# A top-2 MoE router moved ahead of its layer norm: un-normalised logits, an affine part applied at the gathers' copies, and 20 weight places in place of 23

## The chip, the cores and the metric

One core of one Trainium2 chip runs the whole network in one launch. The metric is device microseconds of that launch. The engines are PE (TensorE: matmuls, transposes), DVE (VectorE), ACT (ScalarE), POOL (GpSimd) and SP, whose queue here only issues weight loads from HBM.

## The reference, cut to what matters

Two layers of mixer, layer norm, mixture of experts and layer norm, then two other blocks (a recurrent and a sliding-window one, each with a dense FFN), which the change does not touch. T = 256 tokens, D = 1024, 16 experts of width 512, all in fp32.

```python
mix = hybrid_mixer(x, ...)                    # ends in  concat(heads) @ w_o
x = layer_norm(ALPHA * x + mix, ln1_g[l], ln1_b[l])
aff = sigmoid(x @ router_w)                   # 16 affinities for each token
biased = aff + router_bias
# best group of 4 by the sum of its two largest, then the two largest in that group
gates = chosen affinities over their sum
out = sum over the chosen experts of  gate * (silu(x @ w_gate[e]) * (x @ w_up[e])) @ w_down[e]
x = layer_norm(ALPHA * x + out, ln2_g[l], ln2_b[l])
```

## The kernel before, in words

Tokens stand in two blocks b of 128 rows, and an fp32 product is made from high and low fp32r parts (`xh`, `xl`; `wh`, `wl`): three matmuls for one. `mm` (L174) issues every matmul, `tr` (L228) every transpose.

**The mixer's end.** `down` multiplies the heads with `w_o` into four PSUM tiles `y[b][q]`, q being a half of 512 columns, one after the other. `layer_norm` (L362 for all DVE work) adds the residual, takes moments, and applies scale, gain and bias in two SCALAR_TENSOR_TENSOR passes for each (b, q). `xT_part` transposes the normalised `xn` on PE (`pt`) and splits it into `xh` (ACT, L332) and `xl` (DVE, L333). `warm` (L224) issues matmuls on constants to keep PE at work; twelve stand here.

**The router.** `logits` (`plt`) multiplies `xh`, `xl` with the split router weights `rwhl`; the 32x128 result is copied (`lg`, L838), turned and added up by one small matmul (`psg`), and goes through the sigmoid (L861), the bias add on DVE (L862) and some 25 small DVE instructions to a 0/1 choice `selb` (L886). PE counts ranks in each expert from it (`prk`), DVE forms a one-hot matrix `P` (L1023) of 64 slots for each expert.

**The experts.** Meanwhile ACT and POOL write the split of `xn` with strided columns, `xnh` (L980) and `xnl` (L981). `slots(g)` gathers the tokens of four experts: eight PSUM tiles `pg`, each of four matmuls of `P` with `xnh`, `xnl`, copied out in turn by DVE (L1037) and ACT (L1035) into `xTe`; then four `pgt` transposes and eight `pgs` matmuls. The four PSUM tiles of tag "pb" rotate under all of these. Then for eight pairs p of experts: `gate_up(p)` (`pgg`, `pgu`), `down()` of the pair before (`pdn`), `turn` (`pat`), `spread` (`py`, the sum in four PSUM tiles that begin as ALPHA times `xn`, written by four ACT instructions, L989). `slots(1)` to `slots(3)` stand between the pairs. PE's order there is the program's (`manual_schedule`).

**The weights.** A layer has 96 chunks of 1 MB, each two SP loads of 512 KB (`chunks`, L147). One string says where the first go, ahead of need:

```python
FILL = "rrrmr76rr54rr321rrp0ppx"
LATE = 18
```

Here `r` is a ring buffer, a digit a place of its own, `p` a pair of `xh`, `xl` buffers (three pairs rotate), `m` the tile `misc`, `x` the tile `xn`. That is 23 chunks; `m` holds the fourth chunk in use and is loaded after 18 others. From then on the 18 places of `r` and the digits are used in a cycle, each as soon as its chunk has been multiplied. SP issues strictly in order.

Of the kernel before, what the change touches and what calls it, by code (L numbers as in the profile page):

```python
# [19 lines left out]
D = 1024  # L20
# [13 lines left out]
WARM_LN = 12  # L34
# [63 lines left out]
class Net:  # L98
# [4 lines left out]
    FILL = "rrrmr76rr54rr321rrp0ppx"  # L103
# [153 lines left out]
    def more_consts(s):  # L257
# [8 lines left out]
        s.col = s.cp.tile([128, 32], F32, name="col")  # L266
        t = s.raw()
        rows, rw = t[:32, 0:128], t[:, 128:256].rearrange("p (k e) -> p k e", k=8)
# [4 lines left out]
        rv = A["router_w"].rearrange("(k p) e -> p k e", p=128)  # L273
        for k in (0, 4):
            nc.gpsimd.dma_start(rw[:, k:k + 4], rv[:, k:k + 4])
        return rows, rw

    def columns(s, rows, rw):
        nc = s.nc
        p = s.pb()  # L280
        keep = s.tc.keep_in_program_order
        keep(s.tr(p[:, :27], rows[:27]))
        keep(nc.vector.tensor_copy(s.col[:, :27], p[:, :27]))
        s.rwhl = s.cp.tile([128, 8, 32], F32R, name="rwhl")
        h = s.rwhl[:, :, 0:16]
        keep(nc.scalar.activation(h, rw, AF.Copy))
        keep(nc.vector.tensor_tensor(s.rwhl[:, :, 16:32], rw, h.bitcast(F32), op=ALU.subtract))
# [60 lines left out]
    def layer_norm(s, y, gb, out=None, added=False, after0=None):  # L348
# [38 lines left out]
        with s.tc.high_priority():  # L387
# [6 lines left out]
            if after0:  # L394
                s.warm(WARM_LN)
            else:
                lows((0, 0), (0, 1))
            for q in range(2):
                affine(1, q)
            if after0:  # L400
                lows((0, 0), (1, 0), (0, 1))
                after0()
                lows((1, 1))
            else:
                lows((1, 0), (1, 1))
# [115 lines left out]
    def mixer(s, li):  # L521
# [6 lines left out]
        with ExitStack() as es:  # L528
# [26 lines left out]
            place([128, 1152], "gap2", 1)  # L555
# [12 lines left out]
            for i in range(2):  # L568
                nc.gpsimd.dma_start(alb[64 * i:64 * i + 4], A["alib"][i])
            if li == 0:  # L570
                rows = s.more_consts()
# [35 lines left out]
            if li == 0:  # L607
                s.columns(*rows)
# [156 lines left out]
            gb = s.load_gb(mp, A["ln1_g"][li], A["ln1_b"][li], "kT")  # L765
# [5 lines left out]
            s.lg = []  # L771
            s.down(mh, ml, A["w_o"][li], 8, gb,
                   after0=lambda: s.lg.append(s.logits(0)))

    def down(s, mh, ml, w, nk, gb, col=None, out=None, hold=4, after0=None, pre=None, pool=()):
# [24 lines left out]
        if out is None:  # L800
            s.xh, s.xl = s.new_xT()
# [6 lines left out]
        s.layer_norm(y, gb, out, after0=after0)  # L808
# [19 lines left out]
    def logits(s, b):  # L828
# [4 lines left out]
        for k in range(8):  # L833
            s.mm(p, s.rwhl[:, k], s.xh.k(k, t), k == 0, False)
        for k in range(8):
            s.mm(p[:16], s.rwhl[:, k, 0:16], s.xl.k(k, t), False, k == 7)
        lg = s.st.tile([32, 128], F32, tag="lg", name="lg", bufs=2)
        s.nc.vector.tensor_copy(lg, p)  # L838
        return lg

    def router(s, mp):
# [12 lines left out]
        v.memset(pick, -BIG_NEG)  # L854
        v.memset(gs[:, 0], BIG_NEG)
        s.tc.keep_in_program_order(nc.scalar.activation(sm[:, 0], s.eps, AF.Sigmoid))
        s.lg.append(s.logits(1))
        p = s.pb("psg")
        for b in range(2):
            s.mm(p[:, b * 16:(b + 1) * 16], s.lg[b], s.two, True, True)  # L860
        nc.scalar.activation(R[:, 0], p[:, :32], AF.Sigmoid)  # L861
# [47 lines left out]
        return ga, ov, rs, cnt  # L909

    def overflow(s, li, ga, ov, rs, cnt, xnh, xnl, py):
# [7 lines left out]
        with s.tc.If(n > 64), ExitStack() as es:  # L919
# [4 lines left out]
            for c in range(8):  # L924
# [5 lines left out]
                v.tensor_copy((x0, x1)[c // 4][:, c % 4], p[:, :T])  # L930
# [27 lines left out]
    def moe(s, li, pre):  # L958
        nc, A = s.nc, s.A
        v = nc.vector  # L960
        with ExitStack() as es:
# [14 lines left out]
            keep = s.tc.keep_in_program_order  # L976
            for b in range(2):
# [498 lines left out]
```

## Time and profile before

| what | value |
|---|---|
| median of 3 runs | 1370.97 us (1370.66 to 1371.42) |
| the profiled execution's own time | 1371.13 us |
| its span | 1369.5 us |
| mean granted clock of TensorE | 0.983 |
| PE busy | 1306.6 us (95%) |
| DVE, ACT, POOL busy | 763.1, 583.2, 81.0 us |
| moved from HBM | 340 MB, 249 GB/s on the mean |

Times in rows count from the span's start. The router of layer 0 lies between 126 and 162 us, its experts between 162 and 370; layer 1's router ends 362 us later. A row gives a start, a duration, the engine, the line, what is written and from what, the shapes, how many instructions were merged, and in brackets the idle time before it on its engine with what ended that.

### The profile page before, as it was taken

The page shows a single profiled execution, that of the slowest core. Times are in us where ns is not written, and L with a number is a line of the kernel's source. Part 1 is how long each engine was busy: PE and PEld are TensorE (multiplying, and loading weights), DVE is VectorE, ACT ScalarE, POOL GpSimd, SP SyncE. Part 2 cuts the span into 40 slices and gives each one's busy share as a digit, 9 for nine tenths or more (in the row PEclk, how much of TensorE's full clock was granted, in tenths as well). Part 3 has the DMA queues.
Part 4 walks back from the last instruction along what each step waited for, and adds up shares of the span by engine and source line. Part 5 has one row for each costly group of instructions (what it writes and reads, how often), then busy time and mean ns, then how long its engine had stood idle before and what let it go on. Part 6 is the DMA issues. An engine that isn't in the chain of part 4 may idle for free.

```text
span 1369.5 us, 20419 instructions
## 1 busy us (share of the span) xinstructions
PE 1306.6 (95%) x7941; PEld 955.6 (70%) x7941; DVE 763.1 (56%) x1584; ACT 583.2 (43%) x1110; POOL 81.0 (6%) x90
## 2 busy tenths in 40 slices
PE   7899899999998998999998999999999999999997
PEld 6787443444487664434435888889998887899986
DVE  4775510111368562111115678879886678888845
ACT  5684410101256841101103524556665376566642
POOL 3000100000200010000002143000000010000000
PEclk9999999999999999999999999999999999999999
DMA  9566699999981767999998820466554365575500
GB/s 299 192 236 256 240 408 398 416 418 416 324 304 70 277 244 290 393 416 417 417 416 290 287 96 29 157 214 214 185 202 136 126 216 171 181 234 185 199 18 31
DMA packets 153448, 342.93 MB, mean 250 GB/s; under 512 B 13282, under 2 KB 84840, under 8 KB 153345
## 3 DMA queue, kind: packets, MB, share of 16 engines
q1 hardware_dynamic: 149408, 330.14, 65.4%
q0 software_dynamic: 3616, 11.15, 2.4%
q8 instruction: 66, 1.08, 0.3%
q10 hardware_dynamic: 320, 0.26, 0.1%
q14 instruction: 38, 0.30, 0.1%
HBM read 340.44 MB, written 1.07 MB: 249 GB/s over the span
## 4 chain that ended last, share of the span: by engine, by line
PE 52%; DVE 3%; ACT 1%; issue 1%; DMA 0%; POOL 0%; DVEq 0%; ACTq 0%
PE pb L174 20%; PE y L174 12%; PE pv L174 3%; PE pdn L174 3%; PE pgg L174 3%; PE pgu L174 3%; PE pl L174 2%; PE ptk L174 2%; DVE xn L362 1%; PE py L174 1%; PE pkv L174 1%; PE po L174 1%; PE pt L228 1%; PE pg L174 1%; DVE wl L168 1%
## 5 line engine op out<-in xcount | busy, mean ns | idle before, releaser
L168 DVE TENSOR_TENSOR wl<-raw,wh 128x1024 fp32r<-128x1024 f32 (+1 forms) x208 | 248.3, 1199 | 86.2 <-ACT wh L167 84.3
L167 ACT ACTIVATE wh<-raw 128x1024 fp32r<-128x1024 f32 (+1 forms) x208 | 213.7, 1035 | 70.2 <-PE y L174 62.1
L1067 DVE SCALAR_TENSOR_TENSOR misc<-misc,gs,pgu 128x512 f32<-128x512 f32 x16 | 12.0, 747 | 226.8 <-PE pgu L174 149.8
L174 PE MATMUL pb<-xh,wh 128*128 128x256 f32 (+1 forms) x944 | 133.6, 281 | 0.5 <-ACT wh L167 0.5
L174 PE MATMUL pb<-xh,wl 128*128 128x256 f32 (+1 forms) x944 | 132.5, 281 | 1.6 <-DVE wl L168 1.6
L174 PE MATMUL pb<-xl,wh 128*128 128x256 f32 (+1 forms) x944 | 132.5, 280 | 0.0
L174 PEld LDWEIGHTS pb<-xh,wh 128*128 128x128 f32 (+1 forms) x944 | 120.3, 187 | 2.1 <-ACT wh L167 0.7
L174 PEld LDWEIGHTS pb<-xh,wl 128*128 128x128 f32 (+1 forms) x944 | 119.9, 187 | 2.2 <-DVE wl L168 2.0
L174 PEld LDWEIGHTS pb<-xl,wh 128*128 128x128 f32 (+1 forms) x944 | 119.9, 187 | 0.1
L174 PE MATMUL pgu<-raw,xTe 128*64 128x512 f32 x512 | 112.6, 592 | 0.0
L174 PE MATMUL pdn<-raw,misc 128*64 128x512 f32 x496 | 109.6, 592 | 0.0
L174 PE MATMUL pgg<-raw,xTe 128*64 128x512 f32 x448 | 103.0, 612 | 4.9 <-PEq L919 4.9
L167 ACT ACTIVATE xh<-pdn 128x512 fp32r<-128x512 f32 x32 | 19.1, 597 | 195.6 <-PE pdn L174 195.6
L174 PEld LDWEIGHTS pgu<-raw,xTe 128*64 128x64 f32 x512 | 37.7, 137 | 72.2 <-issue 68.7
L174 PEld LDWEIGHTS pdn<-raw,misc 128*64 128x64 f32 x496 | 36.4, 137 | 69.4 <-issue 64.4
L174 PEld LDWEIGHTS pgg<-raw,xTe 128*64 128x64 f32 x448 | 32.8, 140 | 65.1 <-issue 58.7
L168 DVE TENSOR_TENSOR xl<-pdn,xh 128x512 fp32r<-128x512 f32 x32 | 21.9, 686 | 100.4 <-ACT xh L167 88.5
L174 PE MATMUL y<-wl,gh 128*128 128x512 f32 x176 | 68.7, 390 | 0.0
L174 PE MATMUL y<-wh,gl 128*128 128x512 f32 x176 | 68.6, 390 | 0.0
L174 PE MATMUL y<-wh,gh 128*128 128x512 f32 x176 | 68.2, 389 | 0.0
L1066 ACT ACTIVATE misc<-pgg 128x512 f32<-128x512 f32 x16 | 9.6, 597 | 128.0 <-PE pgg L174 128.0
L174 PE MATMUL y<-wh,xl 128*128 128x512 f32 x128 | 51.4, 403 | 0.0
(357 smaller groups left out, 2267.1 us busy)
## 6 DMA issues: line engine op xcount, KB each, us to landing
raw<-in_w_up SPq DMA_DIRECT2D x128, 512.0 KB, 9.9
raw<-in_w_down SPq DMA_DIRECT2D x124, 512.0 KB, 9.9
raw<-in_w_gate SPq DMA_DIRECT2D x112, 512.0 KB, 10.0
raw<-in_ffn_w_in SPq DMA_DIRECT2D x44, 1024.0 KB, 6.0
raw<-in_ffn_w_out SPq DMA_DIRECT2D x22, 1024.0 KB, 5.1
raw<-in_hgrn_w_in SPq DMA_DIRECT2D x16, 1024.0 KB, 8.4
raw<-in_w_o SPq DMA_DIRECT2D x8, 1024.0 KB, 11.4
raw<-in_w_in SPq DMA_DIRECT2D x6, 1024.0 KB, 7.9
```

The source lines that it names most:

```text
L167: nc.scalar.activation(h, src, AF.Copy)
L168: (nc.gpsimd if pool else nc.vector).tensor_tensor(l, src, h.bitcast(F32), op=ALU.subtract)
L174: s.last = s.nc.tensor.matmul(out, lhsT, rhs, start=start, stop=stop, skip_group_check=True).ins
L228: return s.nc.tensor.transpose(out, in_, s.ident[:k, :k])
L362: prev.append(f(*a, **k).ins)
L1066: nc.scalar.activation(sg, ps[0], AF.Silu)
L1067: v.scalar_tensor_tensor(ac, sg, gs[:, p:p + 1], ps[1], op0=ALU.mult, op1=ALU.mult)
```

## The change

The logits are taken from the residual sum before its norm. With r = 1/std, m the mean and w the router's weights, x.w = r (u.(g w) - m sum(g w)) + sum(b w) for u the un-normalised row; the change centres g w over the rows, so that the mean drops out, and the affinity is sigmoid(r * logit + rc) with rc = sum(b w).

- `layer_norm` is not called at the mixer's end (`down` returns `y`). `router` makes the residual sum, the moments, and the transposes of the un-normalised rows as soon as each `y[b][q]` is there; one order is forced for its DVE and ACT instructions (`seq`).
- `router_weights` forms the centred weights in each layer's mixer (seven DVE instructions, one 128x256 matmul `prw`, one ACT split and its DVE subtraction), from two POOL loads of `router_w`.
- ACT normalises without gain and bias (one 128x1024 Identity for each block) and writes `xnh`; POOL makes `xnl` of block 0 in one instruction, DVE that of block 1 in two halves, after `P`.
- Gain and bias are applied where `slots` copies `pg` out (TENSOR_SCALAR, or Identity with column operands `gp`); `slots` works in two groups of four PSUM tiles, in each first three matmuls for every tile, then the four with `xnl` of block 1.
- The start of `py` (residual) comes from eight DVE instructions after `slots(0)`, with `ln1_g` and `ln1_b` broadcast to 128 rows in a `xh`, `xl` pair, which the ACT queue loads (2 x 512 KB); before, POOL loaded them in the mixer.
- The twelve warm matmuls are gone, and `FILL` loses its last `p` and `x`.

The diff's core:

```diff
-    FILL = "rrrmr76rr54rr321rrp0ppx"
+    FILL = "rrrmr76rr54rr321rrp0p"
...
+    def router_weights(s, li, t):
...
+        for i, d in enumerate((gw, bw)):
+            v.tensor_tensor(d, rw, s.ln1(li, i)[:, :, None].to_broadcast([128, 8, 16]), op=ALU.mult)
+        p = s.pb("prw")
+        s.mm(p[:, :256], ones, t[:, 128:384], True, True)
+        v.tensor_reduce(sums, p[:, :256].rearrange("p (a k e) -> p a e k", a=2, k=8), axis=AX.X, op=ALU.add)
+        v.tensor_copy(s.rc, sums[:, 1])
+        v.tensor_scalar(sums[:, 0], sums[:, 0], 1.0 / D, None, op0=ALU.mult)
+        v.tensor_tensor(gw, gw, sums[:, 0, None, :].to_broadcast([128, 8, 16]), op=ALU.subtract)
...
-            gb = s.load_gb(mp, A["ln1_g"][li], A["ln1_b"][li], "kT")
+            s.router_weights(li, rw)
...
+        def moments(b, q):
+            x = s.xn[:, b, q * 512:(q + 1) * 512]
+            seq(v.scalar_tensor_tensor, x, x, ALPHA, y[b][q], op0=ALU.mult, op1=ALU.add)
...
+            seq(act, h, pv, AF.Copy)
+            seq(v.bn_stats, st[b][:, q], x)
+            if q:
+                seq(v.bn_aggr, mv[b][:, 0:2], st[b])
+                seq(act, mv[b][:, 2:3], mv[b][:, 1:2], AF.Sqrt, bias=s.eps[:, 0:1])
+            return lambda: seq(v.tensor_tensor, l, pv, h.bitcast(F32), op=ALU.subtract)
...
+        def scales(b):
+
+            seq(v.reciprocal, mv[b][:, 3:4], mv[b][:, 2:3])
+            seq(v.scalar_tensor_tensor, mv[b][:, 4:5], mv[b][:, 0:1], -1.0, mv[b][:, 3:4], op0=ALU.mult, op1=ALU.mult)
+
+        def affinity(b):
+            lg = s.st.tile([32, 128], F32, tag="lg", name="lg", bufs=2)
+            seq(v.tensor_copy, lg, s.logits(b, xh, xl))
+            p = s.pb("psg")
+            with s.tc.issue_after(last_y):
+                s.mm(p[:, :16], lg, s.two, True, True)
+            seq(v.scalar_tensor_tensor, aff[:, b], p[:, :16], mv[b][:, 3:4], s.rc, op0=ALU.mult, op1=ALU.add)
...
+            affinity(0)
+            s.tc.keep_in_program_order(low_rows(nc.gpsimd, 0, slice(0, 8)))
+            low = moments(1, 1)
+            seq(act, sm[:, 0], s.eps, AF.Sigmoid)
+            gb = [x.rearrange("p a b -> p (a b)").bitcast(F32) for x in s.pair()]
+            for x, a in zip(gb, (s.A["ln1_g"][li], s.A["ln1_b"][li])):
+                seq(nc.scalar.dma_start, x, bass.AP(tensor=a.tensor, offset=a.offset, ap=[[0, 128], [1, D]]))
+            low()
+            scales(1)
+            affinity(1)
+            seq(act, aff, aff, AF.Sigmoid)
+            normalized(1)
...
+                        v.scalar_tensor_tensor(x, x, ALPHA, gb1[0][:, c], op0=ALU.mult, op1=ALU.mult)
+                        v.scalar_tensor_tensor(py[b][dh], gb1[1][:, c], ALPHA, x, op0=ALU.mult, op1=ALU.add)
...
+                for c0 in range(0, 8, 4):
+                    ps = [s.pb("pg") for _ in range(4)]
+
+                    for bs in ((0, xnh), (0, xnl), (1, xnh)), ((1, xnl),):
+                        for c in range(c0, c0 + 4):
+                            for b, x in bs:
...
+                        if c % 2:
+                            nc.scalar.activation(xt[:, c], p, AF.Identity, scale=ga_, bias=be)
+                        else:
+                            i = v.tensor_scalar(xt[:, c], p, ga_, be, op0=ALU.mult, op1=ALU.add).ins
```

How instructions moved, at three places. **PE at the router's logits.** Before, all of it stands behind the last `y` matmul and the twelve warm ones:

```order
L174 MATMUL py<-mgtb,negI 128x512
L228 MATMUL pt<-c,xn 128x128 x8
L174 MATMUL plt<-xh,rwhl 32x128 x8
L174 MATMUL plt<-xl,rwhl 16x128 x8
L174 MATMUL plt<-xh,rwhl 32x128 x8
L174 MATMUL plt<-xl,rwhl 16x128 x8
L174 MATMUL psg<-c,lg 128x16 x2
L224 LDWEIGHTS negI
```

In the changed kernel, from the third `pt` (block 1, first half) on; the first two stand further up, among the `y` matmuls:

```order
L227 MATMUL pt<-c,xn 128x128 x4
L173 MATMUL plt<-xh,rwhl 32x128 x8
L173 MATMUL plt<-xl,rwhl 16x128 x8
L173 MATMUL y<-wl,xh 128x512
L173 MATMUL y<-wh,xl 128x512
L173 MATMUL y<-wh,xh 128x512
L173 MATMUL y<-wl,xh 128x512
L173 MATMUL y<-wh,xl 128x512
```

Block 0's logits now stand inside the last `y` tile's products. After these come three `py` matmuls that zero PSUM, and then

```order
L173 MATMUL psg<-c,lg 128x16
L227 MATMUL pt<-c,xn 128x128 x4
L173 MATMUL plt<-xh,rwhl 32x128 x8
L173 MATMUL plt<-xl,rwhl 16x128 x8
L173 LDWEIGHTS negI
L173 MATMUL py<-mgtb,negI 128x512
L173 MATMUL psg<-c,lg 128x16
L223 LDWEIGHTS negI
```

so that only block 1's second half of the transposes and its logits are left behind the last `y` product. **DVE around the logits**, the changed kernel, from block 1's first `xl` to the bias add (L885 is `seq`'s line; R holds the affinities):

```order
L885 TENSOR_TENSOR xl<-pt,xh 128x4x128
L885 COPY lg<-plt 32x128
L885 SCALAR_TENSOR_TENSOR R<-psg,mv,rc 128x16
L885 SCALAR_TENSOR_TENSOR xn<-xn,y 128x512
L885 BN_STATS bst<-xn 128x6
L885 BN_AGGR mv<-bst 128x2
L885 TENSOR_TENSOR xl<-pt,xh 128x4x128
L885 RECIPROCAL mv<-mv 128x1
L885 SCALAR_TENSOR_TENSOR mv<-mv 128x1
L885 COPY lg<-plt 32x128
L885 SCALAR_TENSOR_TENSOR R<-psg,mv,rc 128x16
L948 TENSOR_TENSOR R<-R,rb 128x32
```

The last residual sum (`xn<-xn,y`) stands behind block 0's affinity, and the bias add right behind block 1's. **SP at the end of layer 0's fill.** Loads take eight completion semaphores in turn, named DMAHW0 to DMAHW7, and SP issues a load when the load that used its semaphore before has landed. Before:

```order
L147 DMA raw<-in_w_down 128x1024 [waits DMAHW5_49,DVE_49]
L147 DMA raw<-in_w_down 128x1024 [waits DMAHW6_49]
L147 DMA raw<-in_w_down 128x1024 [waits DMAHW7_49,DVE_49]
L147 DMA raw<-in_w_down 128x1024 [waits DMAHW0_49]
L147 DMA xh<-in_w_down 128x1024 [waits DMAHW1_49,PE_49]
L147 DMA xl<-in_w_down 128x1024 [waits DMAHW2_49,PE_49]
L147 DMA misc<-in_w_gate 128x1024 [waits DMAHW3_49]
L147 DMA misc<-in_w_gate 128x1024 [waits DMAHW4_49]
```

Now, the same eight loads; the ACT queue's two broadcast loads (`ln1_g`, `ln1_b`) hold DMAHW0 and DMAHW2 ahead of them:

```order
L146 DMA raw<-in_w_down 128x1024 [waits DMAHW7_49,DVE_49]
L146 DMA raw<-in_w_down 128x1024 [waits DMAHW0_49]
L146 DMA raw<-in_w_down 128x1024 [waits DMAHW1_49,DVE_49]
L146 DMA raw<-in_w_down 128x1024 [waits DMAHW2_49]
L146 DMA xh<-in_w_down 128x1024 [waits DMAHW3_49,DVE_49,PE_49]
L146 DMA xl<-in_w_down 128x1024 [waits DMAHW4_49,PE_49]
L146 DMA misc<-in_w_gate 128x1024 [waits DMAHW5_49]
L146 DMA misc<-in_w_gate 128x1024 [waits DMAHW6_49]
```

The second row here waits for the broadcast load of `ln1_g`, and everything below it in SP's queue with it.

## Rows read from the trace of the kernel before

**Rows 1.** Page, parts 1 and 2: busy times; GB/s in 40 slices of 34 us.

```profile
PE 1306.6 (95%) x7941; PEld 955.6 (70%) x7941; DVE 763.1 (56%) x1584; ACT 583.2 (43%) x1110; POOL 81.0 (6%) x90
...
GB/s 299 192 236 256 240 408 398 416 418 416 324 304 70 277 244 290 393 416 417 417 416 290 287 96 29 157 214 214 185 202 136 126 216 171 181 234 185 199 18 31
```

**Rows 2.** Chain of waits, layer 1's experts: start, duration, what.

```profile
617.08 3.74 PE pg L174 x32
...
621.90 7.02 PE pgg L174 x32
```

**Rows 3.** Windows: stretch, busy time of each engine, PEclk, DMA share, GB/s.

```profile
148.00:156.00 8.00, 3.24 (x14) 1.16 (x13) 5.92 (x32) 3.47 (x7) 3.11 (x2) 0.77 0.99 368
156.00:166.00 10.00, 10.00 (x65) 7.66 (x65) 3.10 (x10) 2.13 (x5) 0.00 (x0) 0.85 0.08 18
```

**Rows 4.** Timeline of layer 0's router, all engines.

```profile
138.28 0.69 DVE L362 SCALAR_TENSOR_TENSOR xn<-xn,y 128x512 f32<-128x512 f32 x1
...
138.51 2.75 PE L224 MATMUL warm<-mgtb,negI 128*128 128x512 bf16 x12
...
145.32 5.78 POOL L981 TENSOR_TENSOR xnl<-xn,xnh 128x1024 fp32r<-128x1024 f32 x2 [55.38 <-PE plt L174]
...
149.26 0.18 ACT L861 ACTIVATE R<-psg 128x32 f32<-128x32 f32 x1
...
149.47 1.69 DVE L862 TENSOR_TENSOR R<-R,rb 128x32 f32<-128x32 f32 x1 [2.24 <-ACT R L861]
...
151.19 0.18 DVE L867 TENSOR_TENSOR pr<-R 128x24 f32<-128x24 f32 x1
```

**Rows 5.** Timeline of PE, layer 0, from the choice to the experts.

```profile
154.27 0.23 PE L174 MATMUL prk<-selb,mgtb 128*128 128x16 bf16 x2 [4.76 <-DVE selb L886]
...
156.14 0.56 PE L174 MATMUL pg<-P,xnh 128*128 128x256 f32 x1
156.50 0.41 PE L174 MATMUL pg<-P,xnl 128*128 128x256 f32 x1
...
162.47 1.08 PE L174 MATMUL pgg<-raw,xTe 128*64 128x512 f32 x4
```

**Rows 6.** Timeline of DVE and PE, layer 1's router.

```profile
512.11 1.74 DVE L862 TENSOR_TENSOR R<-R,rb 128x32 f32<-128x32 f32 x1 [2.22 <-ACT R L861]
...
518.42 0.56 PE L174 MATMUL pg<-P,xnh 128*128 128x256 f32 x1
```

**Rows 7.** Timeline of DVE and POOL at layer 1's second norm.

```profile
732.72 5.53 POOL L217 TENSOR_TENSOR raw<-raw 128x1024 fp32r<-128x1024 f32 x2 [24.37 <-ACT raw L215]
...
733.38 2.65 DVE L362 SCALAR_TENSOR_TENSOR xn<-xn,mv,gb 128x512 f32<-128x512 f32 x1
735.95 0.74 DVE L362 SCALAR_TENSOR_TENSOR xn<-py,mv,gb 128x512 f32<-128x512 f32 x1
```

**Rows 8.** Tile `pg`, 590 to 725 us: ns min/median/max, first and last start.

```profile
L1037 DVE COPY xTe<-pg x8: 424/424/426, 617.6 to 671.6; 128x256 f32<-128x256 f32 x8
L1035 ACT ACTIVATE xTe<-pg x8: 384/385/385, 618.1 to 672.1; 128x256 f32<-128x256 f32 x8
```

**Rows 9.** Timeline of SP's queue, layer 0: issue times.

```profile
138.88 0.90 SPq L147 DMA_DIRECT2D misc<-in_w_gate  x2
...
164.45 0.80 SPq L147 DMA_DIRECT2D raw<-in_w_gate  x2
```

**Rows 10.** DMA issues in small windows (138, 85 to 125, 345 us): KB each, us to landing.

```profile
xh<-in_w_down SPq DMA_DIRECT2D x1, 512.0 KB, 3.7
...
gb<-in_ln_b POOLq DMA_DIRECT2D x1, 512.0 KB, 9.6
...
raw<-in_w_down SPq DMA_DIRECT2D x1, 512.0 KB, 12.6
```

**Rows 11.** Timeline of SP and PE, the end of layer 0's chunks.

```profile
338.60 6.43 SPq L147 DMA_DIRECT2D raw<-in_w_down  x6
...
359.44 7.09 PE L174 MATMUL pdn<-raw,misc 128*64 128x512 f32 x32
```

More of the change, by code (lines that the diff above doesn't have):

```diff
@@ L346, in load_gb, with layer_norm @@
         return gb
-    def layer_norm(s, y, gb, out=None, added=False, after0=None):
+    def layer_norm(s, y, gb, out=None, added=False):
         nc, v = s.nc, s.nc.vector
@@ L607, in mixer @@
             if li == 0:
-                s.columns(*rows)
+                s.columns(rows)
             def index_scores(b):
@@ L770, in mixer, with down @@
             s.attn_out(pp3, lambda j, sb: dv[:, sb], mh, ml, 6, mp)
[L771 to L775, printed above, removed]
+            return s.down(mh, ml, A["w_o"][li], 8, None)
+    def down(s, mh, ml, w, nk, gb, col=None, out=None, hold=4, pre=None, pool=()):
         y = [[s.pa("y") for _ in range(2)] for _ in range(2)]
@@ L799, in down @@
                             mul(k, tb, q, H, L)
-        if out is None:
+        if out is None and gb is not None:
             s.xh, s.xl = s.new_xT()
@@ L833, in logits, with router @@
         for k in range(8):
-            s.mm(p, s.rwhl[:, k], s.xh.k(k, t), k == 0, False)
+            s.mm(p, s.rwhl[:, k], xh.k(k, t), k == 0, False)
         for k in range(8):
[L836 to L841, printed above, removed]
+            s.mm(p[:16], s.rwhl[:, k, 0:16], xl.k(k, t), False, k == 7)
+        return p
+    def router(s, li, mp, y, xnh, xnl):
         nc = s.nc
@@ L853, in router @@
         sm = mp.tile([128, 3, 2], F32, name="sm")
[L854 to L861, printed above, removed]
+        st = [s.st.tile([128, 2, 6], F32, tag="bst", name="bst", bufs=2) for _ in range(2)]
@@ new lines, in normalized, with low_rows @@
+        def normalized(b):
+            x = s.xn[:, b]
+            seq(act, x, x, AF.Identity, scale=mv[b][:, 3:4], bias=mv[b][:, 4:5])
+            seq(act, xnh[:, b].rearrange("p (c q) -> p c q", c=8), x.rearrange("p (q c) -> p c q", c=8), AF.Copy)
+        def low_rows(e, b, c):
+            n, h, l = (t[:, b].rearrange(f, c=8)[:, c] for t, f in ((s.xn, "p (q c) -> p c q"),
+                                                                 (xnh, "p (c q) -> p c q"), (xnl, "p (c q) -> p c q")))
+            return e.tensor_tensor(l, n, h.bitcast(F32), op=ALU.subtract)
@@ new lines, in router @@
+        with s.tc.high_priority():
+            low = [moments(0, 0), moments(0, 1)]
+            for f in low:
+                f()
+            scales(0)
+            low = moments(1, 0)
+            normalized(0)
+            seq(v.memset, pick, -BIG_NEG)
+            seq(v.memset, gs[:, 0], BIG_NEG)
+            low()
[6 more added lines that the diff above has]
+                seq(nc.scalar.dma_start, x, bass.AP(tensor=a.tensor, offset=a.offset, ap=[[0, 128], [1, D]]))
+            low()
+            scales(1)
+            affinity(1)
+            seq(act, aff, aff, AF.Sigmoid)
+            normalized(1)
@@ L1097, in moe @@
             with s.tc.manual_schedule(engines={mybir.EngineType.PE}):
-                slots(0)
+                P, i = onehot(0)
+                with s.tc.issue_after(i):
+                    for c in (0, 4):
+                        low_rows(v, 1, slice(c, c + 4))
+                with s.tc.issue_after(slots(0, P)):
+                    residual()
                 for p in range(8):
```

130 lines of the change are left out of this document (74 added, 56 removed).

## The prediction

> **What bounds the kernel now.** I read the page first, then the chain of waits, the windows, and the timelines around the router. PE is busy 95% of the span [rows 1], so what counts is where PE waits, where it runs at the lower clock, and what is added to its own work. The experts are bound by PE: in the chain of waits the 32 `pg` matmuls of a `slots` call take 3.74 us with nothing between them, and the call 4.82 us from its start to the next `pgg` (617.08 to 621.90) [rows 2]. The load queue runs beside it at 416 to 418 GB/s [rows 1], which is 1.255 us for 512 KB.
>
> The router is bound by a chain of small steps. The sigmoid comes at 149.26; the bias add begins at 149.47 and takes 1.69 us for 32 columns, where its neighbour on 24 columns takes 0.18; it ends at 151.16, just after POOL's two `xnl` instructions at 151.10 [rows 4]. In layer 1 it takes 1.74 us [rows 6]. The same is to be seen at another norm: while POOL works, a DVE instruction on 512 columns takes 2.65 us, and its neighbour with one operand from PSUM 0.74 [rows 7]. So the bias add waits for POOL. PE meanwhile idles 4.76 us before `prk`, and `slots(0)` then takes 6.33 us (156.14 to 162.47) where `slots(1)` took 4.82, its first matmuls at 0.41 us [rows 5]. The granted clock is 0.77 of full over 148 to 156 and 0.85 over 156 to 166 [rows 3]; between the levels 1.2 and 2.4 GHz that is about 6.7 us at 1.2 GHz, after PE's idling, and costs 1.5 us.
>
> **The change, part by part.** The end of the bias add, in layer 0. PE has 4 transposes and block 0's 16 `plt` matmuls more ahead of its last `y`; by the durations of the same instructions today that is 0.6 and 1.05 us, and the last `y` ends at 139.9 instead of 138.25 (the residual sum after it starts at 138.28 [rows 4]). Three `py` matmuls follow, shaped like the warm ones of 0.23 us (2.75 for 12 [rows 4]), and `psg`, and DVE, in its forced order, can add up the last residual only after block 0's affinity, that is at 141.2. From there, by the durations of the same instructions in that timeline: sum 0.69 [rows 4], transposes 0.6, `xh` 0.6, square root 0.3, `xl` and two 128x1 instructions, to 144.1. Here POOL comes in again: its one `xnl` instruction, half of the 5.78 us [rows 4], runs from about 141.85 (when ACT has block 0's `xnh`) to 144.75, and the second 128x1 instruction, whose operands are in SBUF, waits for it as the bias add does now. Then `lg`, `psg`, affinity, sigmoid and bias add, 1.7 us with their hand-overs: 146.45 against 151.16. I take a gain of 4.7 us in each layer (layer 1's rows are alike), 5.4 if the small instruction is not held up, 3.7 if each hand-over costs 0.1 more.
>
> The Trainium skill, page "SBUF — State Buffer", section "SBUF: two separate sides", says that VectorE with two SBUF inputs and GpSimd share a port pair that whichever starts first holds for its whole instruction. By that rule the 1.69 us are a lock, which the trace agrees with, and the gain is the 4.7; with bandwidth merely shared it would be 5.4.
>
> From the bias add to `pg` it is 4.98 us now in layer 0 and 4.57 in layer 1 (513.85 to 518.42) [rows 5, 6]; the instructions there stay, and block 1's `xnl` on DVE comes behind `P` and is needed only by the thirteenth matmul. That I cost at nothing: two instructions of some 0.7 us lie under twelve matmuls of at least 0.117 us each, and what is left over is in the bubbles below. `selb` then comes at 149.55, 3.1 us after the bias add as now; the eight warm matmuls (1.85 us after `psg`, at 145.6) end at 147.5; PE idles 2.05 us where it idled 4.76 [rows 5]. The clock's 1.5 us are then kept in full or lost in full; between these ends I take 0.6 us of gain a layer, the share by which the idling shrinks.
>
> `slots` pays. Now `pg` tiles are done one by one and their copies (0.424 on DVE, 0.385 on ACT [rows 8]) hide under the next tile. In the new order a group's four tiles end within 0.5 us of each other; PSUM has four such tiles, so the second group's first matmul waits for the copy of the first group's first tile, and `pgt` for that of the second's. Each time about 0.38 us (copy and hand-over, less the three matmuls that still run) of PE idling shows: 0.75 us a call, and four calls in a layer, 3.0 us. The bounds are 0 and 1.6 a call (both engines' two copies, twice). `gate_up` starts on the first of the tiles, so the last copies cost nothing more.
>
> `prw`: one fp32 matmul of 128x256. The trace has no such one; the nearest is 0.28 us for `pg` at full clock. Between 0.1 and 1.1 (four passes) I take 0.4 a layer, on PE's path, since the mixer keeps PE busy. Its DVE and ACT work, some 2.5 us, lies beside the `w_o` splits where DVE is about half idle: nothing, or 1 us if `y` waits for a split.
>
> The residual's eight DVE instructions (one like them is the 0.74 us of [rows 7]) take 6 us after `slots(0)`, when DVE next has work 14 us later (two `pgg`/`pgu` turns [rows 2]); the four ACT instructions that go were not awaited by PE. Nothing. The twelve warm matmuls stood before transposes that waited for DVE; nothing either. Two more constant loads lie at the kernel's start: nothing.
>
> **The load queue** moves. SP's loads from the second half of chunk 16 on (11 of them, layer 1: 9) now wait for the broadcast loads, since these take their turn in the completion semaphores. ACT issues them after the sigmoid table, at about 145. A 512 KB load on a quiet queue landed in 3.7 us [rows 10], so SP goes on at 148.7, where `misc` is issued at 138.88 now [rows 9]. `misc` is the seventh behind: 148.7 + 2.5 + 7 x 1.255 = 160.0. It is the fourth chunk; `gate_up` starts at about 157.7 and reaches it 5.2 us later (three quarters of a 7 us `pgg` [rows 2]), at 162.9: 2.9 us to spare. The eleven are through at 165, when the first ring place comes free (now 164.45, 2 us after the first `pgg` [rows 5, 9]). Two chunks fewer are prefetched: four loads, 5.0 us, plus 1 us of delay. The last chunk lands now at 344.7 + 12.6 = 357.3 [rows 10, 11] and is needed when three quarters of the last `pdn` are over, at 359.44 + 5.3 = 364.7 [rows 11]: 7.4 us to spare. Less 6.0, plus the 2.4 us by which PE gets slower after `gate_up`'s start, some 3.8 stay. So no wait.
>
> The sum, a layer: -4.7 - 0.6 + 3.0 + 0.4 = -1.9; two layers -3.8. Against the profiled execution's own 1371.13 (span 1369.5) that is 1367.3; the median shown is 0.16 lower, so 1367.2.
>
> **The rivals.** *No change that can be measured* (under 0.2%, 2.7 us): the bubbles are nearer 1.2 us a call, since DVE also holds two `xnl` halves and the one-hot ahead of its copies, and the clock stays low as long as today: +1.8 and +0.6 a layer, 1371.13 + 1.0, about 1372. For it: every copy of a group starts within half a microsecond. Against: the copies alternate between two engines.
>
> *Slower*: the held load queue decides. Today's broadcast loads, on POOL, took 9.6 us under load [rows 10]. If ACT's take as long, SP goes on at 154.6, `misc` lands at 165.9 against 162.9, and PE stands 3.0 us in layer 0; the last chunks lose what was left of the 3.8. In layer 1 `misc` is two loads nearer: 0.5 us and again the end. With 1 to 2 us at each end that is +3.5 + 3 on the 1367.2: 1373.7, and with the bubbles of the case above 1378. It begins to cost when the loads land later than 6.6 us after issue. Against: the queue is quiet then, since SP itself waits. The Trainium skill, page "DMA: Bandwidth & Descriptors", section "Issuing engines are not separate DMA queues", says that loads from several engines share the same DMA engines; by it the two broadcasts meet only each other here, and no row shows an ACT load of this size.
>
> *More gain*: PE does not fall to 1.2 GHz (another 0.9 a layer) and the bubbles hide in part (0.35 a call, 1.6 a layer): 1367.2 - 5.0, about 1362. For it: 2.05 us of idling where 4.76 went before.
>
> That the logits would not come earlier, the scheduler having put them last, the order rules out.
>
> **How the numbers follow.** Forecast 0.40, no change 0.25, slower 0.17, more gain 0.18. The forecast's own bounds (gain 3.7 to 5.4, bubbles) give 1364.5 to 1370; a tenth of it lies above 1368.2. Faster by over 0.2% (under 1368.2): 0.36 + 0.18 and a little of the no-change case, 0.55; within: 0.27; slower (over 1373.7): 0.18. The range reaches to the rivals' nearer parts, 1361.5 to 1374.5.
>
> **What would show it.** The bias add some 146.5 and 0.2 us long in layer 0; before it a 128x1 DVE instruction stretched to POOL's end; PE idle about 2 us ahead of `prk`; in every `slots` call two gaps of 0.3 to 0.5 us put down to `xTe`; SP silent from about 124 to 148.7, `misc` landed by 160; no PE wait for a load in the experts; the last chunk some 4 us ahead of need. It is wrong if `pgg` or `pdn` wait for a load, if the gaps in `slots` come to over 1.2 us a call, or if the mixer's `y` got longer by over 1 us.

## The result: 0.5% slower, and the profile after

| | before | after |
|---|---|---|
| median of 5 runs each | 1370.97 us (1370.47 to 1371.74) | 1380.07 us (1376.14 to 1380.82) |
| ratio | | 1.0054 [1.0042, 1.0066] |
| profiled execution, its span | 1371.13, 1369.5 us | 1376.56, 1374.9 us |
| mean granted clock | 0.983 | 0.986 |

The forecast was 1367.2, the range ended at 1374.5. The profiled execution is one of two at 1376; the other three lie at 1380.1 to 1380.8 with a mean clock of 0.982 or 0.983, so the traces compared here hold 5.4 us of the 9.1 between the medians.

Line numbers of after are those of the changed kernel: `mm` L173, the weight splits L166 and L167, `chunks` L146, `router_weights` from L303, `seq` L885. The program cut at the same matmuls in both traces (start to start, us):

| stretch | layer 0 | layer 1 | forecast of the difference |
|---|---|---|---|
| start (layer 1: first `pk`) to first `y` | +1.85 | 94.46 -> 101.86 | +0.4 |
| first `y` to last `y` | 30.50 -> 33.58 | 31.61 -> 32.52 | +1.65 |
| last `y` to `prk` | 16.44 -> 9.63 | 16.46 -> 10.01 | -6.35 |
| `prk` to `slots(0)` | 1.87 -> 1.16 | 1.46 -> 1.16 | -0.6, with the next |
| `slots(0)` to `pgg` | 6.33 -> 6.56 | 6.14 -> 6.48 | +0.75 |
| `slots(1)`, (2), (3) | 5.32, 4.92, 4.92 -> 6.73, 6.05, 6.04 | the same within 0.01 | +0.75 each |
| last `pgg` group to last `pdn` | 54.76 -> 54.78 | 54.75 -> 55.16 | 0 |

The first row of layer 0 holds the kernel's first loads too, and these differ from execution to execution (run 5). From the first query projection (`pq`) to the first `y` it is 74.17 -> 76.43, 2.26 us more.

The last `pdn` of layer 0 is 1.44 us late, that of layer 1 5.98. One turn between `slots(1)` and `slots(2)` of layer 1 is 1.4 us shorter than before: there the granted clock fell in the trace of before and did not in that of after (windows before, then after, PEclk third from the end).

```profile
592.00:600.00 8.00, 7.89 (x30) 3.14 (x32) 0.00 (x0) 0.00 (x0) 0.00 (x0) 0.79 1.03 413
```

```profile
592.00:600.00 8.00, 5.44 (x28) 3.08 (x28) 1.91 (x3) 0.60 (x1) 0.00 (x0) 1.00 1.02 406
```

PE idles in this turn in both, 2.3 and 2.6 us. Runs 1 and 2, with the same experts as after, have the fall: it is the luck of an execution, not the change's doing.

**The router did what the forecast said** [rows 4, 5]. Its timeline in layer 0:

```profile
139.51 0.16 DVE L885 SCALAR_TENSOR_TENSOR mv<-mv 128x1 f32<-128x1 f32 x1
...
144.95 2.91 POOL L925 TENSOR_TENSOR xnl<-xn,xnh 128x1024 fp32r<-128x1024 f32 x1 [116.38 <-ACT xnh L885]
...
147.24 0.63 DVE L885 SCALAR_TENSOR_TENSOR mv<-mv 128x1 f32<-128x1 f32 x1
...
149.08 0.19 DVE L948 TENSOR_TENSOR R<-R,rb 128x32 f32<-128x32 f32 x1 [0.30 <-ACT R L885]
...
152.40 0.21 PE L173 MATMUL prk<-selb,mgtb 128*128 128x16 bf16 x2 [2.05 <-DVE selb L972]
```

The bias add takes 0.19 us where it took 1.69. POOL's hold has moved to the 128x1 instruction: block 0's takes 0.16, block 1's 0.63, and ends at 147.87 with POOL (144.95 + 2.91). PE idles 2.05 us ahead of `prk`. That this is the forecast to the hundredth is luck, the forecast being a difference of two estimated times; layer 1 has 1.5.

The windows, with the layout of [rows 3]; the third one is layer 1's mixer:

```profile
148.00:156.00 8.00, 5.71 (x35) 3.63 (x35) 6.83 (x38) 3.82 (x5) 0.00 (x0) 1.00 0.87 302
156.00:166.00 10.00, 9.40 (x56) 5.35 (x58) 8.00 (x17) 3.62 (x6) 0.00 (x0) 1.00 1.02 401
387.00:400.00 13.00, 7.67 (x49) 7.47 (x48) 6.26 (x15) 3.59 (x9) 0.00 (x0) 0.74 1.06 370
```

After 2.05 us of idling the clock stays at 1.00 in layer 0's router (0.77 and 0.85 before). But `slots(0)` doesn't get shorter by it. Nor is the clock sure: in other runs with the same router `prk` to `pgg` takes 7.6 to 7.7 us, or 8.8 to 8.9 where the clock falls (run 4 in both layers, run 1 in layer 1).

**`slots` pays more than forecast.** The copies of tile `pg` in layer 1 (min, median, max), which answer [rows 8], and then what PE waits for in layer 0's experts (in all, times, longest):

```profile
L1133 DVE TENSOR_SCALAR xTe<-pg,gp x8: 532/542/549, 621.9 to 677.2; 128x256 f32<-128x256 f32 x8
L1131 ACT ACTIVATE xTe<-pg,gp x8: 556/561/565, 622.1 to 677.3; 128x256 f32<-128x256 f32 x8
```

```profile
PE pgt L227 <- DVE xTe L1133: 1.2, 4, 0.3
PE pg L173 <- DVE xTe L1133: 0.9, 3, 0.3
```

With the column operands a copy takes 0.54 us on DVE and 0.56 on ACT, against 0.424 and 0.385, and shows at both places the forecast named, the second group's first matmul and `pgt`. The waits list 0.3 us for each. From start to start it is 0.57 us at each place where these matmuls else follow every 0.117, and 0.1 more goes at the second matmul of the new group. A call is 1.1 to 1.4 us longer, not 0.75.

**The mixer pays what was costed at nothing.** Layer 1, before the first split that PE waits for: POOL, DVE and PE of after, then DVE of before.

```profile
382.42 0.80 POOL L283 DMA_DIRECT2D gap<-in_router_w  x1 [4.65 <-DVE xn L389]
385.08 0.78 POOL L283 DMA_DIRECT2D gap<-in_router_w  x1 [1.86 <-issue]
...
391.28 0.49 DVE L305 TENSOR_TENSOR gap<-gap,col 128x128 f32<-128x128 f32 x2 [6.90 <-DMA gap<-in_router_w]
...
392.38 4.16 DVE L167 TENSOR_TENSOR wl<-raw,wh 128x1024 fp32r<-128x1024 f32 x5
...
386.87 1.46 PE L173 MATMUL pb<-xh,wh 128*128 128x256 f32 x11
393.65 2.08 PE L173 MATMUL pb<-xh,wl 128*128 128x256 f32 x8 [5.33 <-DVE wl L167]
```

```profile
386.33 4.16 DVE L168 TENSOR_TENSOR wl<-raw,wh 128x1024 fp32r<-128x1024 f32 x5
```

The loads of `router_w` go out only at 382.42 and 385.08. The first waits 4.65 us for the norm of the layer before (L389), by my reading of the program because `gap` takes memory that was the norm's. The second lands at 391.19. DVE stands 6.90 us in front of `router_weights`' first product, and the `wl` splits queue behind it: 392.38 against 386.33. PE idles 5.33 us, and the clock then falls (0.74 over 387 to 400).

In layer 0 the loads are there in time, but the attention's order on PE is another one. 64-column matmuls there start two at a time when PE's order puts two groups next to each other. Before, then after, in the same stretch:

```profile
102.99 0.88 PE L174 MATMUL po<-pT,V 128*64 128x256 f32 x8
```

```profile
103.55 0.86 PE L173 MATMUL po<-pT,V 128*64 128x256 f32 x4
...
104.97 0.86 PE L173 MATMUL po<-pT,V 128*64 128x256 f32 x4
```

Eight took 0.88 us as neighbours, and now two groups of four 0.86 each. By the starts of single matmuls, 12 pairs of the 48 `po` matmuls from 90 us on ran side by side before, and 4 now. From `pq` to the first `y` it is 2.26 us more, and the `y` stretch is 1.43 longer than its 1.65 us of inserted work explains. In layer 1 the order came out the other way: 8 pairs before and 12 now, and the `y` stretch grows by 0.91 us, 0.74 less than the inserted work.

**SP's queue** [rows 9] stood as forecast:

```profile
126.17 25.61 SPq L146 DMA_DIRECT2D raw<-in_w_down  x4
...
152.85 1.04 SPq L146 DMA_DIRECT2D misc<-in_w_gate  x2
```

The second of these four was held to 150.20 (forecast 148.7, with the broadcast loads issued 1 us later than thought), and by the waits of SP's queue it was held by the load of `ln1_g`:

```profile
SPq L146 <- DMA xh<-in_ln_g: 23.7, 1, 23.7
```

`misc` landed at 162.97, 2.86 us after `pgg` began (160.11) and 2.3 before its need. PE waits for no load in layer 0's experts: from `pgg` to `slots(1)` it is 36.61 us, before 36.62. But the last load lands 203.9 us after `pgg`'s start, 9.0 later than before; 6.0 was the forecast. In layer 1 the last `pdn` group but one (a group is the 32 matmuls of a pair) takes 7.43 us where 7.04 is its length. By the order of the loads, its last load landed only 0.56 us before the matmul that reads it began.

### The profile page after: what moved, and what is told of

It is laid out like the page before. It is cut to its first block, busy times and chain, and to the rows that moved or that the text cites. A ratio compares the mean times of both kernels' runs of the same rounds, so it can differ in the third digit from the quotient of the medians.

```text
span 1374.9 us, 20368 instructions
## 1 busy us (share of the span) xinstructions
PE 1306.5 (95%) x7921; PEld 954.6 (69%) x7921; DVE 769.9 (56%) x1611; ACT 588.1 (43%) x1107; POOL 77.0 (6%) x90
## 4 chain that ended last, share of the span: by engine, by line
PE 49%; DVE 4%; DMA 2%; ACT 1%; issue 1%; POOL 0%; DVEq 0%; ACTq 0%; SPq 0%
PE pb L173 19%; PE y L173 12%; PE pv L173 3%; PE pgg L173 3%; PE pgu L173 2%; PE pdn L173 2%; PE pl L173 2%; PE ptk L173 2%; DVE xn L389 1%; DMA raw<-in_w_down 1%; DMA raw<-in_hgrn_w_in 1%; PE pkv L173 1%; DVE wl L167 1%; PE po L173 1%; PE pt L227 1%
## 5 line engine op out<-in xcount | busy, mean ns | idle before, releaser
L167 DVE TENSOR_TENSOR wl<-raw,wh 128x1024 fp32r<-128x1024 f32 (+1 forms) x208 | 248.3, 1199 | 88.1 <-ACT wh L166 86.0
L166 ACT ACTIVATE wh<-raw 128x1024 fp32r<-128x1024 f32 (+1 forms) x208 | 213.7, 1035 | 69.9 <-PE y L173 63.5
L173 PE MATMUL pb<-xh,wl 128*128 128x256 f32 (+1 forms) x944 | 133.4, 282 | 6.2 <-DVE wl L167 6.2
L173 PE MATMUL pb<-xh,wh 128*128 128x256 f32 (+1 forms) x944 | 133.9, 282 | 0.5 <-ACT wh L166 0.5
L173 PE MATMUL pb<-xl,wh 128*128 128x256 f32 (+1 forms) x944 | 133.3, 281 | 0.0
L173 PEld LDWEIGHTS pb<-xh,wl 128*128 128x128 f32 (+1 forms) x944 | 120.7, 188 | 6.8 <-DVE wl L167 6.7
L173 PEld LDWEIGHTS pb<-xh,wh 128*128 128x128 f32 (+1 forms) x944 | 120.8, 188 | 2.1 <-ACT wh L166 0.7
L173 PEld LDWEIGHTS pb<-xl,wh 128*128 128x128 f32 (+1 forms) x944 | 120.8, 188 | 0.1
L173 PE MATMUL pgg<-raw,xTe 128*64 128x512 f32 x480 | 108.1, 603 | 5.2 <-PEq L1005 5.2
L173 PE MATMUL pgu<-raw,xTe 128*64 128x512 f32 x512 | 112.6, 592 | 0.0
L173 PE MATMUL pdn<-raw,misc 128*64 128x512 f32 x496 | 110.0, 593 | 0.0
L166 ACT ACTIVATE xh<-pdn 128x512 fp32r<-128x512 f32 x32 | 19.1, 597 | 196.0 <-PE pdn L173 196.0
L173 PEld LDWEIGHTS pgu<-raw,xTe 128*64 128x64 f32 x512 | 37.7, 137 | 72.2 <-issue 68.7
L173 PEld LDWEIGHTS pdn<-raw,misc 128*64 128x64 f32 x496 | 36.6, 137 | 69.6 <-issue 67.7
L173 PEld LDWEIGHTS pgg<-raw,xTe 128*64 128x64 f32 x480 | 34.6, 138 | 68.9 <-issue 58.6
L167 DVE TENSOR_TENSOR xl<-pdn,xh 128x512 fp32r<-128x512 f32 x32 | 22.0, 686 | 101.1 <-ACT xh L166 101.0
L173 PE MATMUL y<-wl,gh 128*128 128x512 f32 x176 | 68.7, 390 | 0.0
L173 PE MATMUL y<-wh,gl 128*128 128x512 f32 x176 | 68.6, 390 | 0.0
L173 PE MATMUL y<-wh,gh 128*128 128x512 f32 x176 | 68.2, 389 | 0.0
L173 PE MATMUL y<-wl,xh 128*128 128x512 f32 x128 | 51.5, 404 | 0.0
```

The source lines that it names most:

```text
L166: nc.scalar.activation(h, src, AF.Copy)
L167: (nc.gpsimd if pool else nc.vector).tensor_tensor(l, src, h.bitcast(F32), op=ALU.subtract)
L173: s.last = s.nc.tensor.matmul(out, lhsT, rhs, start=start, stop=stop, skip_group_check=True).ins
```

## The experiments

Twelve runs, each beside runs of before on its own chips (median there 1371.5 to 1372.3). The theories: the new work in the mixer costs the time (the wait for `router_w` and the order of PE); or the hold of SP's queue by the broadcast loads does; later, that the stream of expert weights is a second bound right behind PE.

**1. `router_w` loaded once, with the constants, into a tile of its own**

```diff
+        s.rwc = s.cp.tile([128, 8, 16], F32, name="rwc")
...
-        rw, gw, bw, ones = e3(0), e3(128), e3(256), t[:, 384:512]
+        rw, gw, bw, ones = s.rwc, e3(128), e3(256), t[:, 384:512]
...
-            s.router_rows(rw)
```

> The changed kernel with router_w kept in a tile of its own, loaded once at the start; nothing is loaded for the router in the mixers. Theory A (the loss is in the mixers: in layer 1 a DVE multiplication waits 6.9 us for the load of router_w, and the weight splits behind it on DVE hold PE for 5.3 us and a spell at 1.2 GHz): that wait is gone, about 6.5 us less, 1370 where the profiled execution of the changed kernel had 1376.6; layer 0 as before or up to 3 us either way, if PE's order in its attention comes out otherwise. Theory B (the expert load queue, held behind the broadcast loads, makes the loss): no change, 1376 to 1380.

1373.65 us, ratio 1.0018 [1.0009, 1.0026]. `pk` to first `y` in layer 1 is 95.00 us (after 101.86, before 94.46), and PE's wait at the same place:

```profile
PE pb L173 <- DVE wl L167: 0.7, 1, 0.7
```

So 6.9 us were this wait with the low clock behind it (101.86 less 95.00). Layer 0's mixer stays 3 us late, with the same pairs lost: that is another cause.

**2. The router's weights used as they are, split once at the start**

```diff
...
-            s.router_rows(rw)
...
-            s.router_weights(li, rw)
```

> The changed kernel without the centred router weights: the split of router_w is made once in layer 0 as in the kernel before, gain, centring and the bias row are left out of the logits; all else as changed. Theory A: both the wait in layer 1 (6.5 us) and what the weights' making did to layer 0's mixer (its last w_o product comes 3 us later than its added instructions explain) go: 1376.6 - 6.5 - 3 = 1367. Theory B: 1376 to 1380. If layer 0's mixer stays late here, its order was changed by something else than the weights: 1370.

1370.49 us, ratio 0.9997 [0.9988, 1.0006]: some 10 us off after's median. Layer 1 has 94.51 from `pk` to `y`. In layer 0 the 12 `po` pairs are back, `pq` to `y` is 74.40 us, and the `y` stretch is 32.55 us, 1.0 less than after's. In layer 1 the pairs fall to 8 again, and its `y` stretch is 33.57, 1.05 more than after's. The instructions of `router_weights` thus shift PE's order in the attention too, not only wait; in the `y` stretches of the two layers together the shift comes to nothing.

**3. `slots(1)` to `slots(3)` tile by tile, as before**

```diff
+                    todo_ = [(bs, c) for bs in (...) for c in range(c0, c0 + 4)]
+                    if g:
+                        todo_.sort(key=lambda z: z[1])
...
```

> The changed kernel with the gather's matmuls of the second to fourth call of each layer tile by tile again (four for a tile, then the next), the copies with gain and bias as changed; the first call keeps its groups. If the groups cost the gaps in front of the fifth tile and of the transposes, about 1.0 us a call by the changed kernel's trace, six calls: 6 us less, 1370.5. If the slower copies (0.54 and 0.56 us where 0.42 and 0.385 were) set the pace in either order: no change, 1376 to 1380.

The calls take 5.27, 4.92, 4.92 us again, so the order alone makes the bubbles; the slow copies are hidden then. That is 3.7 us a layer, but the time is 1377.93, ratio 1.0046 [1.0033, 1.0059]. The last stretch of the experts grows from 54.78 to 59.76 us in layer 0 and to 56.83 in layer 1. All of the 5 us in layer 0 go in the last `pdn` group but one (11.43 us from its first start to its last, 6.44 in after). PE and its weight loads (PEld) now wait for chunks (waits of layer 0's experts, then of 306 to 372 us), and the chain of waits runs through the loads:

```profile
PE pdn L173 <- DMA raw<-in_w_down: 1.2, 4, 0.4
```

```profile
PEld pdn L173 <- DMA raw<-in_w_down: 6.2, 7, 1.3
```

```profile
333.06 10.21 DMA raw<-in_w_up
343.28 12.97 DMA raw<-in_w_down
362.55 6.21 PE pdn L173 x28
```

What PE gains, the load stream takes back: it is the next bound.

**4. The broadcast loads on POOL's queue**

```diff
-                seq(nc.scalar.dma_start, x, bass.AP(...))
+                seq(nc.gpsimd.dma_start, x, bass.AP(...))
```

> The changed kernel with the two broadcast loads of ln1's gain and bias issued by the POOL queue, whose completion semaphores the expert loads do not use. Theory B: the expert loads go on at 127 us again in place of 150, and what PE lost goes: 5 us or more less. Theory A: PE waits only some 0.4 us for the fourth chunk in layer 0, so 0 to 0.5 us less; POOL's block-0 subtraction and its load issues stand in one queue, which may give 1 us back.

1381.59 us, ratio 1.0070 [1.0058, 1.0083]. SP no longer waits for the broadcast loads. It still waits for the `xh`, `xl` pair:

```profile
SPq L146 <- DVE xl L885: 9.8, 1, 9.8
```

It issues the pair at 148.18 in place of 151.89, `misc` lands 3.7 us ahead of the first `pgg`, and the last load lands 201.9 us after it, 1.9 sooner than in after. Nothing is gained, so the hold is not what made after slower. No row shows the 0.4 us of waiting for the fourth chunk that the expectation gives theory A. The profiled run, 1383.30 us, has a mean clock of 0.983, as after's three higher runs have; its windows around layer 0's router show one place where the clock falls:

```profile
148.00:156.00 8.00, 5.14 (x33) 2.43 (x31) 6.33 (x38) 5.62 (x7) 2.52 (x2) 0.91 0.84 272
156.00:166.00 10.00, 9.29 (x60) 6.94 (x60) 7.38 (x16) 3.92 (x6) 0.00 (x0) 0.90 0.69 266
```

PE is at the lower level for a part of it, and `prk` to `pgg` takes 8.9 us against 7.7. It does so in layer 1 too (8.8). Whether after's three higher runs lost their 4 us there no trace shows.

**5. After, once more**

> The changed kernel itself, on the chip of the next three, as their measure. Theory A and B alike: 1376 to 1381. Up to the gather it should again have PE's wait in layer 1's mixer of 5 us or more in front of the first weight product that needs DVE's split.

1381.44 us (1377.95 to 1383.98), ratio 1.0070 [1.0056, 1.0084]; PE's wait in layer 1's mixer is 5.3 us, as expected. From `pq` on the stretches are those of the first trace within 0.1 us, but for the very last (54.77 for 55.16); the first projections, which wait for the kernel's first loads, are 1.9 us later (`pq` at 34.62 for 32.76). That stretch alone can thus make half of the 4 us between after's lower and higher runs.

**6. Edits 1 and 3 together**

> The changed kernel with router_w resident and the gather of the second to fourth call tile by tile. By theory A with the parts added up: 6.9 us from the wait, 7.3 from the gathers' gaps (3.65 a layer, measured between the calls' first matmul and the next expert's), 1362 to 1366. By theory C (the expert loads are the second bound: the prefetch is two chunks shorter, the queue is held until 150 us, and the last chunk had 2 us to spare where 7.4 were before): what the gathers give is lost again in front of the last chunks, 5 us in layer 0 and 2 in layer 1, as in the tile-order run; about 1371.

1371.01 us, ratio 0.9987 [0.9978, 0.9996]. The last stretches are 58.43 and 56.60 us where 54.8 is PE's own: 3.7 and 1.9 us are lost to the last chunks. With the wait in layer 1's mixer and the calls' 3.7 us a layer given back, loads are the bound at the end of each layer.

**7. Edit 6, and ACT issues the broadcast loads at the router's start**

```diff
+            gb = [...]
+            for x, a in zip(gb, ...):
+                seq(nc.scalar.dma_start, x, bass.AP(...))
             low = [moments(0, 0), moments(0, 1)]
...
-            gb = [...]
-            for x, a in zip(gb, ...):
-                seq(nc.scalar.dma_start, x, bass.AP(...))
```

> As the run before, with the two broadcast loads issued by ACT at the router's start (about 130 us) in place of behind the second table load (146). Theory C: SP goes on with the expert loads at about 137 in place of 150, the loads run ahead by up to 8 us until the ring is full, and the last chunks are there in time: 1364 to 1367, no PE wait for a load in the experts. If the loads' end is set by the two missing places alone: as the run before, 1371.

1373.95 us, ratio 1.0013 [1.0004, 1.0022]. The test spoiled itself: the scheduler put the third `pt` behind all `y` matmuls, and last `y` to `prk` became 15.67 us, so the router's gain was gone. Of the queue it says this much: the last load lands 202.3 us after `pgg`'s start, only 0.8 earlier than in edit 6.

**8. Edit 7, and the router's weights made right behind the query projections**

```diff
                 s.columns(rows)
+            s.router_weights(li, rw)
             def index_scores...
...
-            s.router_weights(li, rw)
```

> As the run before, with the centred router weights made right after the query projections in place of inside the attention. If the weights' instructions there are what put layer 0's products out of their side-by-side order (8 of 12 pairs of the value products, 2 of 14 of the scores lost, 3 us), the pairs are back and it is 2 to 3 us faster than the run before. If the order comes out as it likes with any edit: the same or slower by up to 2 us, with the DVE-bound index stage some 1.5 us longer.

1373.94 us, ratio 1.0016 [1.0007, 1.0025]. The pairs in layer 0 are back (12 again), yet the first `y` comes only 0.5 us sooner after `pq`: the index stage between them is 1.45 us longer, as the expectation's second case has it. Last `y` to `prk` is 15.67 as in edit 7, and the time is the same.

What made the loads late was still open: two chunks' worth of places (23 against 21, which the title counts as 20), the hold, or the loads' own pace. In the saturated stretch a 512 KB load came every 1.256 us before and every 1.280 in all kernels above (medians). By the programs' layout the changed kernels keep their weight places 96 or 64 bytes past a multiple of 512, the kernel before 288 or 256. The next four ran together.

**9. Edit 6, with an unused constant tile of 192 bytes, which puts the places where they were**

```diff
         s.rc = s.cp.tile([128, 16], F32, name="rc")
+        s.cp.tile([128, 48], F32, name="padc")
```

> The resident and tile-order kernel with one unused constant tile of 192 bytes, which moves every weight place so that its address stands to multiples of 512 bytes as in the kernel before (288 and 256 over, where the changed kernels have 96 and 64). Theory D (the expert loads land 1.280 us apart in every changed kernel and 1.256 before because of where the places begin): 1.256 again, the last load lands some 3.5 us sooner after the first expert matmul, PE's wait for the last chunks (3.7 and 1.9 us in the resident and tile-order run) shrinks to under 1; 1366 to 1368. Rival (the slower loads come from the loads' order or the chip): 1.280 stays, no change against 1371.

1364.06 us (1363.84 to 1364.42), ratio 0.9945 [0.9931, 0.9958]: faster than both kernels. From the DMA view of 220 to 320 us, three lines: before, after, and this one.

```profile
DMA packets 11415, 41.64 MB, mean 416 GB/s; under 512 B 1270, under 2 KB 1270, under 8 KB 11408
```

```profile
DMA packets 11205, 40.87 MB, mean 409 GB/s; under 512 B 1248, under 2 KB 1248, under 8 KB 11197
```

```profile
DMA packets 11399, 41.59 MB, mean 416 GB/s; under 512 B 1266, under 2 KB 1266, under 8 KB 11391
```

The pace is back (spacing 1.263), the last load of layer 0 lands 199.5 us after `pgg`'s start in place of 203.1, and the last stretches take 55.13 and 55.59, 4.3 us less than in edit 6 over both layers. Beside before, the median gained 6.5; the other 2 us have no cause shown (the two traces also differ in where the clock fell). Layer 0's mixer is still 3 us late in it.

**10. Before, with an unused tile of 320 bytes, which puts its places at the changed kernel's**

```diff
         s.col = s.cp.tile([128, 32], F32, name="col")
+        s.cp.tile([128, 80], F32, name="padc")
```

> The kernel before with one unused constant tile of 320 bytes, which puts its weight places at the changed kernel's addresses; nothing else. Theory D: loads 1.280 us apart, the last load of a layer 3 us later, still ahead of need (7 us to spare), time within 1 us of before. Rival: 1.256, nothing changes.

1371.8 us, ratio 1.0003 [0.9994, 1.0012]. The DMA view over the same stretch:

```profile
DMA packets 11217, 40.92 MB, mean 409 GB/s; under 512 B 1248, under 2 KB 1248, under 8 KB 11210
```

The spacing is 1.280, and the last load lands 2.5 us later. So the layout by itself makes these loads 2% slower, with no instruction changed; the kernel before has the slack to bear it. The tile moves everything placed behind it; that it is the address of the weight places is argued, not shown.

**11. Before, with 21 places**

```diff
-    FILL = "rrrmr76rr54rr321rrp0ppx"
+    FILL = "rrrmr76rr54rr321rrp0p"
```

> The kernel before with the prefetch string of the changed kernel (21 chunks in place of 23), nothing else. By the prediction's reckoning the last chunk lands 5 us later, 2.4 us ahead of need: no change, 1370.5 to 1372.5. If the two chunks are what made the loads the bound: PE waits for the last chunks, 1 us a layer or more, 1373 or above.

1371.4 us, ratio 1.0001 [0.9992, 1.001]; the last load is 3.6 us later. Of the 9.0 us the places thus make 3.6 and the layout 2.5. Of the 2.9 that are left, run 4 shows 1.9 to be the hold: without it the last load of layer 0 lands that much sooner. Why the last 1.0 is lost is open.

**12. Edit 9, with the broadcast loads in SP's own queue, behind the eleventh fill chunk**

```diff
-                seq(nc.scalar.dma_start, x, bass.AP(...))
+                s.tc.keep_in_program_order(nc.sync.dma_start(x, bass.AP(...)))
```

> The padded kernel with the two broadcast loads put into SP's own queue, between the eleventh and twelfth chunk of the fill, so that no expert load waits for a load of another queue. Theory C: SP no longer stands still from 126 to 150, the fourth chunk is there before 150, and the rest of the lateness goes: last load at 198 to 200 us after the first expert matmul, no wait for a chunk, 1365 to 1367. If the hold costs nothing by then: as the padded run.

1378.19 us, ratio 1.0046 [1.0033, 1.0060]. The waits of SP's queue:

```profile
SPq L946 <- DVE xl L527: 22.7, 1, 22.7
SPq L946 <- PE y L173: 18.9, 1, 18.9
```

SP stood until the `xh`, `xl` pair was free (22.7 us for a DVE instruction of the attention, 18.9 for a `y` product), and all weights behind it. `misc` landed 9.9 us after `pgg` began, and PE paid (waits of layer 0's experts):

```profile
PE pgg L173 <- DMA misc<-in_w_gate: 3.4, 1, 3.4
PE pgg L173 <- DMA raw<-in_w_gate: 2.5, 1, 2.5
```

This is the slower rival's mechanism, made real by a longer hold: a queue held beyond its slack costs what `misc` is late. After's own hold ended in time.

## Why the prediction was wrong

Right were these steps. **The router**: from last `y` to `prk` 6.8 us less in layer 0 and 6.45 in layer 1, forecast 6.35. **POOL's hold**: the forecast let the 128x1 instruction be held to POOL's end, and it took 0.63 us for 0.16, ending with POOL. The Trainium skill, page "SBUF — State Buffer", section "SBUF: two separate sides", gives a lock that VectorE with two SBUF inputs and GpSimd hold for a whole instruction; this trace agrees with it. Also right were **PE's idling** of 2.05 us (by luck so closely), **SP's hold**, `misc` in time, and **no PE wait for a load** in layer 0's experts. **`prw`**: two matmuls a layer of 0.377 us each, started 0.215 us apart, which is about the 0.4 a layer that was taken.

Of the clock the better end came, by luck: no fall in layer 0's router in the profiled run, 1.5 us kept where 0.6 was taken; run 4's profile has the fall. It hid the bubbles of `slots(0)`: 6.56 at full clock against 6.33 with a part at half.

The step that failed is the sentence on `router_weights`: "Its DVE and ACT work, some 2.5 us, lies beside the `w_o` splits where DVE is about half idle: nothing, or 1 us if `y` waits for a split." The work was priced by its durations at the place where the source has it. Its first product stands much further ahead on DVE, in front of the splits of the layer's first projections, and behind two loads, the first of which POOL starts only after the norm of the layer before. That was 6.9 us in layer 1 (run 1). And the other instructions shifted PE's order in layer 0's attention, some 3 us (runs 1 and 2); in layer 1 the same shift gave 0.7 back. Against -3.8 us for the whole sum, these decide its sign. The prediction's own sign of being wrong, the mixer's `y` longer by over 1 us, came true with it.

Two terms were mis-sized. The bubbles, 0.75 us a call, measured 1.1 to 1.4 in calls 1 to 3: 2.8 us more over both layers. The sum had the copies at their old duration, with an upper bound of 1.6 that held. And the load stream's spare, some 3.8 us by the forecast, was 2 in layer 0 of after: the layout, worth 2.5 us, was not thought of. It is also least at the last `pdn` group but one, not at the last one where the forecast took it: 1.9 us in layer 0 and 0.56 in layer 1. In after it cost 0.4 us, in layer 1; but it takes back what any repair of the other terms would give (run 3).

From the forecast's -3.8 us these terms lead to 8.6 (6.9 + 3.0 - 0.7 + 2.8 + 0.4 more). The traces differ by 5.4: before's lost 1.4 by the clock in layer 1, and the router, `slots(0)` and what lies behind the experts came out 1.9 better than forecast. What made three of after's five runs 4 us longer than the profiled one stays open.

The slower rival had the right sign for another reason. Its price came from `misc` and the last chunks, and in after's trace `misc` was not waited for and a chunk by 0.4 us; run 4, without the hold, was no faster.

## What to carry to other kernels

Price a moved or added instruction by where it stands in its engine's queue, by what its own loads wait for and by who is queued behind it, not by its duration at the place where the source has it. Small side work in a stretch where two engines alternate can cost several times its length; if its data is constant, keep it resident. And when a bound is lifted by some microseconds, measure the next one first: here the load stream, 2 us behind, took back most of what the repairs of runs 3 and 6 gave until its own pace was restored.

## What was not expected of the hardware

- The same 512 KB loads from HBM come every 1.256 us or every 1.280 us (416 or 409 GB/s) by the program's layout: places at 288 and 256 bytes past a multiple of 512, or at 96 and 64. Both directions were run (runs 9 and 10). Which of the two offsets matters, and why, is open.
- 64-column matmuls: eight take 0.88 us, and four 0.86, if the four have no partner next to them.
- An idle time of PE of the same length can end with the clock at its lower level or not: behind 2.3 us in before's layer 1 it fell for 3.4 us, behind 2.6 us at the same place in after it stayed at 1.00.
- In some runs (the profiles of runs 1 and 2) the 128x256 matmuls of a dense FFN start every 0.113 us and in others every 0.118, both at a granted clock of 1.00, worth some 4 us by an estimate from the 928 of them. No cause was found, so the stretches were compared only up to the experts' end.
